# The odd mixer in the program's order: recurrence behind its inputs, two convolution blocks between the transform and its inverse

## The chip, the cores and the metric

One core of one Trainium2 chip runs the whole program. The metric is the time of one execution on the device in microseconds. Five engines with a queue of their own each work through their instructions in order and wait for each other by semaphores: TensorE (PE in the profile; PEld is its weight load), VectorE (DVE), ScalarE (ACT), GpSimd (POOL) and SyncE (SP), which issues the transfers.

## What is computed

A two-layer trunk over 256 latent tokens and 256 context tokens, of width 1024. The change touches the mixer of layer 1, the odd one. Half of its channels are a Hyena operator (a gated long convolution by FFT), half a gated linear recurrence in both directions (RG-LRU). In the reference, cut to the recurrence and the odd mixer:

```python
    for dr in range(2):
        r = jax.nn.sigmoid(... w_a[dr] ...)
        ig = jax.nn.sigmoid(... w_x[dr] ...)
        log_a = -LRU_C * r * jax.nn.softplus(-lam[dr].astype(f32))
        a = jnp.exp(log_a)
        b = jnp.sqrt(-jnp.expm1(2.0 * log_a)) * (ig * xc)
        h = linear_scan(a, b, None if h0 is None else h0[dr], reverse=dr == 1)
        y = h if y is None else y + h
    return (y * jax.nn.gelu(u_gate.astype(f32))).astype(u_x.dtype), finals

def odd_mixer(...):
    hy_l, lx_l, lg_l = jnp.split(h_lat @ w_in, cut, axis=-1)
    r_ctx, ctx_finals = rglru_stream(lx_c, lg_c, *lrup, None, need_ctx_out)
    r_lat, _ = rglru_stream(lx_l, lg_l, *lrup, ctx_finals, True)
    y_lat = jnp.concatenate([hyena_stream(hy_l, *hyp), r_lat], axis=-1) @ w_out
```

The Hyena part takes three groups of 512 channels, each through a convolution of three taps, multiplies the second by the third, convolves the product with a long filter (by a Fourier transform, plus a bias times the product), and multiplies by the first.

## The kernel before

Activations lie with channels on the 128 partitions and tokens along the row: 256 columns of context (CTX) and 256 of latent (LAT), T2 = 512. Every product of matrices is made from three passes (`mm3`, lines 160 to 162): inputs and weights are split into a high and a low part. A weight block of 128x1024 is loaded, cast by ScalarE (L150) and subtracted by VectorE (L151), so each of the 24 matmuls of a block of 1024 input channels has its weight ready.

The odd mixer (`odd_mixer`) begins with a norm and the four blocks of the recurrence's input lx (on both halves of the columns, with the depthwise convolution on ScalarE and VectorE), and goes on with 16 blocks of `od_in` on the latent columns alone: four for the gate lg (Gelu, L1197), 32 single passes for the recurrence's gates (L1207, sigmoid L1208), then eight blocks for the two factors x1 and vv of the product uu (`conv`, L1189 to L1191), whose 128x128 pieces are transposed (L1256), and four blocks for x0. ScalarE copies the transposed product (L1278); 20 passes make the forward transform (L1287 to L1292); VectorE multiplies by the filter's transform (L1294 to L1299, twelve operations); 32 passes make the inverse (L1311), and the result is multiplied by x0 and split into a high and a low part. The eight split tiles, four of the recurrence and four of the Hyena part, are the input of `od_out`, 8 blocks of 24 matmuls.

The recurrence is made from 128x512 operations, four tiles for each direction: tanh (L1216), exp (L1221), square (L1222), VectorE's one-minus (L1223), the gate times lx (L1224), the root (L1229), the input product (L1230), and a scan (L1232 for direction 0; two half scans L1235 and L1236 for direction 1, whose latent half starts from the end of the context half). Each step of it is given to the scheduler at a lower priority (`later`), so a scheduler sorts its operations into the queues between the others by its own estimate.

Memory comes from pools of fixed size with tags: x (8 buffers of 4 KB a row), g (8), lx (2), hy (13), w (4 weight blocks), raw (4), mm (6 PSUM banks). A tile that takes a buffer waits until the tile that held it before was last used.

Of the kernel before, what the change touches and what calls it, by code (L numbers as in the profile page):

```python
# [18 lines left out]
P = 128  # L19
# [43 lines left out]
LN_PARTS = _split3(math.log(2.0), 9, 11)  # L63


class Builder:
# [87 lines left out]
    def mm3(self, ps, w, x, first=True, last=True, keep=False):  # L154
        mm = self.nc.tensor.matmul
# [9 lines left out]
    def split(self, hi, lo, src):  # L165
        self.nc.scalar.copy(hi, src)
        self.nc.vector.tensor_sub(lo, src, hi)
# [343 lines left out]
    def unscaled(self, l, k, xs):  # L511
# [559 lines left out]
    def hyena_prepare(self):  # L1071
# [6 lines left out]
        w1, w2, zt = hp[0:33, 4:68], hp[0:64, 68:132], hp[0:33, 132 : 132 + NTOK]  # L1078
        w3 = self.slot("y", [P, 1024])
# [16 lines left out]
        for j in range(2):  # L1096
# [3 lines left out]
            for d in range(2):  # L1100
                ps = self.ps()
                nc.tensor.matmul(ps, lhsT=h1[:, j * P : (j + 1) * P], rhs=w3[0:64, d * HYC : (d + 1) * HYC], start=True, stop=True)
                e.tensor_mul(fl[:, d, :], ps, dec[:, d, :])
            s = self.slot("y", [P, 2, HYC])
# [56 lines left out]
    def odd_mixer(self):  # L1161
# [7 lines left out]
        cw = self.const([P, 12, 4], "hy_cw", t["hy_cw"])  # L1169
        hb = self.const([P, 4], "hy_b", t["hy_b"])  # L1170
# [15 lines left out]

        def conv(i, o):
            p = self.proj("od_in", i, xs, *LAT)[:, N:T2]
            nc.scalar.activation(o, p, AF.Identity, bias=cw[:, i, 3:4], scale=cw[:, i, 1:2])  # L1189
            v.scalar_tensor_tensor(o[:, 1:N], p[:, 0 : N - 1], cw[:, i, 0:1], o[:, 1:N], op0=ALU.mult, op1=ALU.add)  # L1190
            v.scalar_tensor_tensor(o[:, 0 : N - 1], p[:, 1:N], cw[:, i, 2:3], o[:, 0 : N - 1], op0=ALU.mult, op1=ALU.add)  # L1191
            return o

        lg = self.slot("hy", [P, 4, N])
        for i in range(4):
            ps = self.proj("od_in", 16 + i, xs, *LAT)
            nc.scalar.activation(lg[:, i], ps[:, N:T2], AF.Gelu_apprx_tanh)  # L1197
        gates = {}
        for i in range(4):
            if i % 2 == 0:  # L1200
                wg = self.rawp.tile([P, 2, 4, P], F32, tag="raw", name=self.uid("wg"))
                nc.sync.dma_start(wg, t["lru_w"][:, i : i + 2])
            for d in range(2):
                ra = gates[i, d] = self.slot("g", [P, 2, T2])
                for g in range(2):
                    ps = self.pm()
                    nc.tensor.matmul(ps, lhsT=wg[:, i % 2, 2 * d + g, :], rhs=lx[i], start=True, stop=True)  # L1207
                    nc.scalar.activation(ra[:, g], ps, AF.Sigmoid, bias=lp[:, d, g, i : i + 1])  # L1208

        hs = {}  # L1210

        def recur(d):

            aa = [self.slot("hy", [P, 2, T2]) for _ in range(4)]
            for i in range(4):
                nc.scalar.activation(aa[i][:, 1], gates[i, d][:, 0], AF.Tanh, scale=kap[:, d, i : i + 1])  # L1216
            yield
            for i in range(4):
                a, b = aa[i][:, 0], aa[i][:, 1]
                r, ig = gates[i, d][:, 0], gates[i, d][:, 1]  # L1220
                nc.scalar.activation(a, r, AF.Exp, scale=kap[:, d, i : i + 1])  # L1221
                nc.scalar.activation(r, a, AF.Square)  # L1222
                v.scalar_tensor_tensor(b, r, 1.0, b, op0=ALU.add, op1=ALU.mult)  # L1223
                v.tensor_mul(ig, ig, lx[i])  # L1224
# [356 lines left out]
```

## Time and profile before

| | |
|---|---|
| three runs | 1765.29 (median), 1762.47, 1765.68 us |
| the profiled execution | 1764.04 us, span 1762.0 us, mean granted clock 0.99 |
| TensorE busy | 1702.8 us, 97% of the span |
| VectorE, ScalarE, GpSimd busy | 1267.6 (72%), 693.7 (39%), 13.2 us (1%) |
| the odd mixer, from the first latent block of od_in to the end of od_out | 1439.66 to 1558.2 us |

The page gives the busy time of each engine, then the chain that ended last with the share of each engine, and the costliest groups of instructions. The time line lists single instructions: start, duration, engine, line, operation, output and inputs, and in brackets how long the engine was idle before, and what ended that. Waits are the same brackets summed by line. A row for a stretch gives the busy time of every engine in it.

### The profile page before, as it was taken

How to read it: one execution, taken by the hardware profiler on the slowest of the kernel's cores; microseconds unless marked ns; L12 is line 12 of the kernel's file. 1: busy time of each engine (PE TensorE's matmuls, PEld its weight loads, DVE VectorE, ACT ScalarE, POOL GpSimd, SP SyncE). 2: the span in 40 equal slices, each digit the busy share in tenths (PEclk: the TensorE clock that was granted, in tenths of full speed). 3: DMA queues.
4: the chain of work that ended last, by engine and by line, in shares of the span. 5: the costliest groups of instructions: out<-in, count | busy, mean ns of one | idle time of the engine just before them, and what ended most of it. 6: DMA issues, size and time to landing. Idle time of an engine off the chain costs nothing.

```text
span 1762.0 us, 24867 instructions
## 1 busy us (share of the span) xinstructions
PE 1702.8 (97%) x9380; PEld 1443.5 (82%) x9380; DVE 1267.6 (72%) x2545; ACT 693.7 (39%) x1101; POOL 13.2 (1%) x47
## 2 busy tenths in 40 slices
PE   5999999999989999999999999999999999699998
PEld 3788878889878788778888888888888888499998
DVE  7999999987488668776676686555543576976675
ACT  4433333443445654222222233222222357554443
POOL 0000000000000000000000000000000000000000
PEclk9999999999998999999999999999999999899999
DMA  9566767662465453564554443555533225155552
GB/s 330 172 221 213 228 212 229 215 189 95 126 188 166 132 188 107 171 216 147 164 190 157 159 141 124 181 185 155 169 120 96 96 96 187 67 171 189 183 183 90
DMA packets 107480, 292.65 MB, mean 166 GB/s; under 512 B 21152, under 2 KB 35360, under 8 KB 107104
## 3 DMA queue, kind: packets, MB, share of 16 engines
q1 hardware_dynamic: 101504, 286.86, 50.6%
q10 hardware_dynamic: 5216, 2.62, 0.8%
q0 software_dynamic: 640, 1.57, 0.3%
q8 instruction: 74, 1.21, 0.3%
q14 instruction: 46, 0.38, 0.1%
HBM read 272.20 MB, written 18.28 MB: 165 GB/s over the span
## 4 chain that ended last, share of the span: by engine, by line
PE 89%; DVE 6%; DMA 2%; issue 1%; SPq 1%; ACT 1%; DVEq 0%; ACTq 0%
PE mm L160 25%; PE mm L162 25%; PE mm L161 25%; PE mm L157 7%; DVE w L151 1%; DMA h<-in_modw_dram 1%; PE mm L1207 1%; SPq L1040 1%; DMA x<-d_g 1%; PE mm L907 1%; DVE x L322 0%; DVE nt L315 0%; PE mm L191 0%; PE ps L690 0%; PE ps L1118 0%
## 5 line engine op out<-in xcount | busy, mean ns | idle before, releaser
L150 ACT CAST w<-raw 128x1024 fp32r<-128x1024 f32 (+2 forms) x324 | 328.8, 1019 | 530.6 <-PE mm L162 262.2
L161 PE MATMUL mm<-x,w 128*128 128x512 f32 (+1 forms) x1424 | 519.8, 365 | 0.0
L162 PE MATMUL mm<-x,w 128*128 128x512 f32 (+1 forms) x1424 | 519.2, 365 | 0.0
L160 PE MATMUL mm<-x,w 128*128 128x512 f32 (+1 forms) x1424 | 514.6, 367 | 3.5 <-ACT x L320 2.2
L151 DVE TENSOR_TENSOR w<-raw,w 128x1024 fp32r<-128x1024 f32 (+2 forms) x324 | 383.8, 1186 | 150.5 <-ACT w L150 149.3
L160 PEld LDWEIGHTS mm<-x,w 128*128 128x128 f32 x1424 | 267.4, 189 | 49.5 <-ACT x L320 2.5
L161 PEld LDWEIGHTS mm<-x,w 128*128 128x128 f32 x1424 | 268.6, 189 | 43.8 <-issue 2.0
L162 PEld LDWEIGHTS mm<-x,w 128*128 128x128 f32 x1424 | 268.5, 189 | 43.9 <-issue 1.2
L227 DVE CUSTOM_DVE_ANT_0 junk<-m,sc 128x1024 f32<-128x1024 f32 x224 | 273.0, 1219 | 1.8 <-DMA m<-in_modw_dram 0.4
L160 PE MATMUL mm<-h,w 128*128 128x512 f32 x456 | 178.3, 394 | 0.0
L162 PE MATMUL mm<-h,w 128*128 128x512 f32 x456 | 176.9, 390 | 0.0
L161 PE MATMUL mm<-h,w 128*128 128x512 f32 x456 | 176.7, 390 | 0.0
L435 DVE SCALAR_TENSOR_TENSOR res<-mm,mraw,res 128x256 f32<-128x256 f32 x192 | 86.0, 479 | 96.5 <-PE mm L162 87.2
L471 DVE TENSOR_TENSOR h<-h,mm 128x512 f32<-128x512 f32 x66 | 45.3, 686 | 108.1 <-PE mm L162 95.8
L470 ACT ACTIVATE h<-mm 128x512 f32<-128x512 f32 x66 | 39.5, 598 | 196.0 <-PE mm L162 185.2
L160 PEld LDWEIGHTS mm<-h,w 128*128 128x128 f32 x456 | 85.6, 188 | 18.9 <-issue 1.1
L162 PEld LDWEIGHTS mm<-h,w 128*128 128x128 f32 x456 | 85.6, 188 | 18.5 <-issue 0.6
L161 PEld LDWEIGHTS mm<-h,w 128*128 128x128 f32 x456 | 85.6, 188 | 18.4 <-issue 1.0
L160 PE MATMUL mm<-hy,w 128*128 128x258 f32 x352 | 99.2, 284 | 0.7 <-DVE g L499 0.7
L162 PE MATMUL mm<-hy,w 128*128 128x258 f32 x352 | 99.6, 283 | 0.0
L161 PE MATMUL mm<-hy,w 128*128 128x258 f32 x352 | 99.6, 283 | 0.0
L157 PE MATMUL mm<-x,w 128*128 128x256 f32 x384 | 66.3, 290 | 6.7 <-DVE x L322 6.2
(371 smaller groups left out, 2002.1 us busy)
## 6 DMA issues: line engine op xcount, KB each, us to landing
raw<-in_wgu_dram SPq DMA_DIRECT2D x176, 512.0 KB, 3.9
m<-in_modw_dram SPq DMA_DIRECT2D x130, 512.0 KB, 4.3
raw<-in_wd_dram SPq DMA_DIRECT2D x64, 512.0 KB, 3.6
raw<-in_wd_dram SPq DMA_DIRECT2D x32, 384.0 KB, 3.3
raw<-in_od_in_dram SPq DMA_DIRECT2D x20, 512.0 KB, 3.5
h<-in_modw_dram SPq DMA_DIRECT2D x12, 512.0 KB, 10.0
raw<-in_ev_in_dram SPq DMA_DIRECT2D x10, 512.0 KB, 3.5
d_mb<-mbt SPq DMA_DIRECT2D x16, 256.0 KB, 3.4
```

Source lines behind the costliest of these rows:

```text
L150: nc.scalar.copy(hi[:, :n], raw[:, :n])
L151: nc.vector.tensor_sub(lo[:, :n], raw[:, :n], hi[:, :n])
L157: mm = lambda *a, **k: self.keep(self.nc.tensor.matmul(*a, **k))
L160: mm(ps, lhsT=wh, rhs=xh, start=first and i == 0, stop=False)
L161: mm(ps, lhsT=wh, rhs=xl, start=False, stop=False)
L162: r = mm(ps, lhsT=wl, rhs=xh, start=False, stop=last and i == n - 1)
L227: nc.vector.tensor_tensor_reduce(self.junk, w, self.sc[:, v, :], 1.0, 0.0, ALU.mult, ALU.add, raw[:, dt, v : v + 1])
L435: self.nc.vector.scalar_tensor_tensor(r, ps[:, c0:c1], gate[:, i, VEC[h] : VEC[h] + 1], r, op0=ALU.mult, op1=ALU.add)
L470: nc.scalar.activation(s[:, 0, lo:hi], pg[:, lo:hi], AF.Silu)
L471: nc.vector.tensor_mul(s[:, 1, lo:hi], s[:, 0, lo:hi], pu[:, lo:hi])
L907: nc.tensor.matmul(ps, lhsT=q[0:96, c : c + P], rhs=k[0:96, :nk], start=True, stop=True)
L1040: nc.sync.dma_start(uy[g * 16 : (g + 1) * 16, 1, :].rearrange("p (s n) -> p s n", s=L), d_y[i * 8 + g].rearrange("s c n -> c s n"))
```

## The change

The mixer's operations on ScalarE, VectorE and TensorE go through three objects of a new class `InOrder` (A, V, T). Each adds to every instruction a dependence on the one that was issued through it before, without a semaphore, so that the scheduler keeps the program's order on that engine. Weight casts and subtractions (`wload`) do not go through them and are still sorted in by the scheduler. In the changed kernel all these instructions show line 74.

- The steps of the recurrence become functions (`tanhs`, `exps`, `squares`, `one_minus`, `roots`, `inputs`, `scan`), called at written places between the convolution blocks (`half`) and gate blocks (`gate_proj`). The gates are made in pairs between the blocks, and the gate's Gelu is one 128x1024 activation near the end instead of four.
- The transposed product is copied over `uu` instead of into a tile of its own, right after the first block of x0; the forward transform follows conv(1); conv(2) and conv(3) come between it and the inverse. The squares and exponentials of direction 1 are placed ahead of the transform, its one-minus, roots and input products behind the frequency product.
- The Hyena bias is added to the filter's first tap beforehand, so the result of the inverse is only multiplied by x0.
- The eight split tiles come in four rounds, a tile of the recurrence and one of Hyena each; the rows of `od_out` are stored in that order. The first four blocks of od_out (`first`, `grow`) accumulate two tiles after each round; the other four come at the end as before.
- The two shift columns of the next norm's input are split in `done`, tile by tile.

```diff
+class InOrder:
...
+    def __init__(self, tc, eng):
+        self.tc, self.eng, self.last = tc, eng, None
+    def __getattr__(self, name):
+        def call(*a, **k):
+            ins = getattr(self.eng, name)(*a, **k)
+            if self.last is not None:
+                dep = mybir.DependencyInfo(mybir.DependencyClass.NoSync, mybir.DependencyReason.DATA)
+                self.tc.add_manual_dep(ins.ins, self.last, dep, reason="in order")
+            self.last = ins.ins.name
+            return ins
+        return call
...
-        for i, x in enumerate(xs):
-            self.split(x[:, 0, NTOK : NTOK + 2], x[:, 1, NTOK : NTOK + 2], sh[:, i, 0:1].to_broadcast([P, 2]))
+                self.split(x[:, 0, NTOK : NTOK + 2], x[:, 1, NTOK : NTOK + 2], sh[:, i, 0:1].to_broadcast([P, 2]))
...
+        A, V, T = InOrder(self.tc, nc.scalar), InOrder(self.tc, v), InOrder(self.tc, nc.tensor)
...
+        def gate_proj(i):
+            A.copy(lg[:, i], self.proj("od_in", 16 + i, xs, *LAT, eng=T)[:, N:T2])
...
+        def gate(i):
...
+                    T.matmul(ps, lhsT=self.wg[:, i % 2, 2 * d + g, :], rhs=lx[i], start=True, stop=True)
+                    A.activation(ra[:, g], ps, AF.Sigmoid, bias=lp[:, d, g, i : i + 1])
+                V.tensor_mul(ra[:, 1], ra[:, 1], lx[i])
...
+        def tanhs(d):
...
+                aa[i, d] = self.slot("hy", [P, 2, T2])
+                A.activation(aa[i, d][:, 1], gates[i, d][:, 0], AF.Tanh, scale=kap[:, d, i : i + 1])
...
+        def exps(d):
...
+                A.activation(aa[i, d][:, 0], gates[i, d][:, 0], AF.Exp, scale=kap[:, d, i : i + 1])
+        def squares(d):
...
-        def later(k, low):
-            with self.tc.high_priority(offset=-low):
-                for _ in range(k):
-                    next(lru)
+                A.activation(gates[i, d][:, 0], aa[i, d][:, 0], AF.Square)
+        def one_minus(d):
+            for i in range(4):
+                b = aa[i, d][:, 1]
+                V.scalar_tensor_tensor(b, gates[i, d][:, 0], 1.0, b, op0=ALU.add, op1=ALU.mult)
+        def roots(d):
+            for i in range(4):
+                b = aa[i, d][:, 1]
+                A.activation(b, b, AF.Sqrt, scale=-1.0)
+        def inputs(d, i):
+            b = aa[i, d][:, 1]
+            V.tensor_mul(b, b, gates[i, d][:, 1])
+        def scan(d, i):
+            a, b = aa[i, d][:, 0], aa[i, d][:, 1]
+            hh = hs[i, d] = gates[i, d][:, 0]
+            if d == 0:
+                V.tensor_tensor_scan(hh, a, b, 0.0, op0=ALU.mult, op1=ALU.add)
+                return
+            rv = lambda x, c0, c1: x[:, c0:c1][:, ::-1]
+            V.tensor_tensor_scan(rv(hh, 0, N), rv(a, 0, N), rv(b, 0, N), 0.0, op0=ALU.mult, op1=ALU.add)
+            V.tensor_tensor_scan(rv(hh, N, T2), rv(a, N, T2), rv(b, N, T2), hh[:, 0:1], op0=ALU.mult, op1=ALU.add)
...
+        def half(i, k):
+            if k == 0:
+                self.tm = self.slot("hy", [P, 2, N])
+            conv(4 + 4 * k + i, self.tm[:, k])
+            if k:
+                V.tensor_mul(uu[:, i], self.tm[:, 1], self.tm[:, 0])
...
+        gate_proj(0)
+        gate_proj(1)
+        gate(0)
+        gate(1)
+        half(0, 0)
+        half(0, 1)
+        gate(2)
+        gate(3)
+        half(1, 0)
+        tanhs(0)
+        half(1, 1)
+        turn(0)
+        gate_proj(2)
+        exps(0)
+        half(2, 0)
+        turn(1)
+        squares(0)
+        half(2, 1)
+        gate_proj(3)
+        one_minus(0)
+        half(3, 0)
+        turn(2)
+        roots(0)
+        half(3, 1)
...
         for i in range(4):
-            tm = self.slot("hy", [P, 2, N])
-            x1, vv = conv(4 + i, tm[:, 0]), conv(8 + i, tm[:, 1])
-            v.tensor_mul(uu[:, i], vv, x1)
-            if i:
-                turn(i - 1)
-        later(4, 150)
+            inputs(0, i)
+        tanhs(1)
+        for i in range(4):
+            scan(0, i)
...
-        conv(0, x0[:, 0])
-        conv(1, x0[:, 1])
-        turn(3)
-        ut = self.slot("x", [P, 2, HYC])
-        for j in range(2):
-            nc.scalar.copy(ut[:, j, :], pts[j])
-        conv(2, x0[:, 2])
-        conv(3, x0[:, 3])
         idft = self.slot("hy", [P, 4, N])
         nc.sync.dma_start(idft, t["idft"])
+        conv(0, x0[:, 0])
+        turn(3)
+        ut = uu.rearrange("p (j k) n -> p j (k n)", j=2)
+        for j in range(2):
+            A.copy(ut[:, j, :], pts[j])
+        conv(1, x0[:, 1])
+        exps(1)
+        squares(1)
         yr, yi = self.slot("x", [P, 2, HYC]), self.slot("x", [P, 2, HYC])
...
+        conv(2, x0[:, 2])
+        one_minus(1)
+        conv(3, x0[:, 3])
+        roots(1)
+        A.activation(lg, lg, AF.Gelu_apprx_tanh)
...
+            inputs(1, i)
...
+        def lru_out(i):
+            scan(1, i)
+            h0 = hs[i, 0][:, N:T2]
+            V.tensor_add(h0, h0, hs[i, 1][:, N:T2])
+            V.tensor_mul(lg[:, i], lg[:, i], h0)
...
+            self.split(o[:, 0, N:T2], o[:, 1, N:T2], lg[:, i], A, V)
+            return o
...
+        def hy_ps(i):
...
+                T.matmul(ps[:, :N], lhsT=src, rhs=idft[:, f, :], start=f == 0, stop=f == 3)
+            return ps
+        def hy_out(i, ps):
...
+            V.tensor_mul(z, x0[:, i], ps[:, :N])
...
+            self.split(o[:, 0, N:T2], o[:, 1, N:T2], z, A, V)
+            return o
...
+        gate = self.need(1, 5)
+        os = [None] * 8
+        first = [(self.wload(t["od_out"][b], D), self.pm()) for b in range(4)]
+        def grow(b, k, n=1):
+            w, ps = first[b]
+            self.mm3(ps[:, N:T2], self.wparts(w, KT)[k : k + n], self.parts(os[k : k + n], *LAT), k == 0, k + n == KT, eng=T)
+        zs = [hy_ps(0), hy_ps(1)]
+        for i in range(4):
+            os[2 * i] = lru_out(i)
+            os[2 * i + 1] = hy_out(i, zs[i])
+            if i < 3:
+                for b in range(4):
+                    grow(b, 2 * i, 2)
+            if i < 2:
+                zs.append(hy_ps(i + 2))
+        for b in range(4):
+            grow(b, 6, 2)
...
-        self.out_proj("od_out", 1, os, [LAT])
+        for b in range(4):
+            self.residual(b, first[b][1], gate, LAT, True)
+        for b in range(4, KT):
+            w = self.wload(t["od_out"][b], D)
+            ps = self.pm()
+            self.mm3(ps[:, N:T2], self.wparts(w, KT), self.parts(os, *LAT))
+            self.residual(b, ps, gate, LAT, True)
         self.done = None
...
-    o["od_out"] = wtile(cat([w[512:], w[:512]], axis=0))
+    o["od_out"] = wtile(np.stack([w[512:].reshape(4, P, D), w[:512].reshape(4, P, D)], axis=1).reshape(D, D))
```

Three places as the built programs have them. The first is ScalarE's queue around the copies of the transposed product (ps to x before, ps to hy in the changed kernel); hy_12429 and hy_12443 are x0, hy_12383 to hy_12386 the root tiles of direction 0, g tiles hold gates and scans. Before:

```order
L1229 ACTIVATE hy_12383<-hy_12383 128x512
L1189 ACTIVATE hy_12429<-mm_12506,hy_cw 128x256
L1229 ACTIVATE hy_12384<-hy_12384 128x512
L150 CAST w_12800<-raw_12798 128x1024
L1278 COPY x_12498<-ps_12103 128x512
L1278 COPY x_12498<-ps_12104 128x512
L1229 ACTIVATE hy_12385<-hy_12385 128x512
L1189 ACTIVATE hy_12429<-mm_12539,hy_cw 128x256
L150 CAST w_12836<-raw_12834 128x1024
```

In the changed kernel, with a line of dots for the tanh and weight casts between:

```order
L74 ACT_TABLE_LOAD
L74 ACTIVATE hy_12421<-g_11995,kap 128x512
L74 ACTIVATE hy_12423<-g_12011,kap 128x512
...
L74 ACTIVATE hy_12443<-mm_12451,hy_cb,hy_cw 128x256
L74 COPY hy_11920<-ps_11921 128x512
L74 COPY hy_11920<-ps_11922 128x512
L74 ACTIVATE hy_12443<-mm_12488,hy_cb,hy_cw 128x256
```

The copies stood behind the second block of x0, with two roots of direction 0 still to come; now they stand behind the first one, with all roots ahead of them. x0 (hy_12443) takes the buffer of a tile of direction 0, whose scans stand on VectorE (next place).

The second place is VectorE's queue around the first operations of the frequency product (x<-mm, four of the twelve are shown; SCALAR_TENSOR_TENSOR into g with one input is a scan). Before:

```order
L151 TENSOR_TENSOR w_12836<-raw_12834,w_12836 128x1024
L1230 TENSOR_TENSOR hy_12386<-hy_12386,g_12088 128x512
L1232 SCALAR_TENSOR_TENSOR g_12074<-hy_12385 128x512
L1294 TENSOR_TENSOR x_12569<-mm_12571,hy_12423 128x512
L1191 SCALAR_TENSOR_TENSOR hy_12429<-mm_12539,hy_cw,hy_12429 128x255
L1223 SCALAR_TENSOR_TENSOR hy_12599<-g_12051,hy_12599 128x512
L1232 SCALAR_TENSOR_TENSOR g_12088<-hy_12386 128x512
L1223 SCALAR_TENSOR_TENSOR hy_12600<-g_12065,hy_12600 128x512
L1295 TENSOR_TENSOR x_12579<-mm_12572,hy_12424 128x512
L1297 TENSOR_TENSOR x_12570<-mm_12571,hy_12424 128x512
```

In the changed kernel:

```order
L74 SCALAR_TENSOR_TENSOR g_12089<-hy_12159 128x512
L74 SCALAR_TENSOR_TENSOR g_12105<-hy_12161 128x512
L169 TENSOR_TENSOR w_12641<-raw_12639,w_12641 128x1024
L74 SCALAR_TENSOR_TENSOR hy_12443<-mm_12451,hy_cw,hy_12443 128x255 x2
L74 SCALAR_TENSOR_TENSOR hy_12443<-mm_12488,hy_cw,hy_12443 128x255 x2
L74 TENSOR_TENSOR x_12524<-mm_12526,hy_12437 128x512
L74 TENSOR_TENSOR x_12534<-mm_12527,hy_12438 128x512
L169 TENSOR_TENSOR w_12647<-raw_12645,w_12647 128x1024
L74 TENSOR_TENSOR x_12524<-x_12524,x_12534 128x512
L74 TENSOR_TENSOR x_12525<-mm_12526,hy_12438 128x512
L74 TENSOR_TENSOR x_12534<-mm_12527,hy_12439 128x512
L169 TENSOR_TENSOR w_12653<-raw_12651,w_12653 128x1024
```

Scans of direction 0 and one-minus operations of direction 1 (hy_12599, hy_12600) stood between the products; now all scans stand ahead, the taps of x0's first two blocks follow, and then come the products with two weight subtractions between them. The x tiles that the products write (x_12524, x_12525, x_12534) take buffers of the eight x tiles that are the input of conv(2) and conv(3) on TensorE.

The third place is VectorE's queue at the output tiles: g_12051 and others are the half scans of direction 1, hy_11917 (hy_11919) the gate lg, hy_12664 (hy_12674) the product with x0, and the split's subtraction writes g or x. Before:

```order
L1236 SCALAR_TENSOR_TENSOR g_12095<-hy_12602,g_12095 128x256
L1238 TENSOR_TENSOR g_12058<-g_12058,g_12065 128x256
L1238 TENSOR_TENSOR g_12074<-g_12074,g_12081 128x256
L1303 TENSOR_TENSOR hy_11917<-hy_11917,g_12044 128x256
L1238 TENSOR_TENSOR g_12088<-g_12088,g_12095 128x256
L1303 TENSOR_TENSOR hy_11917<-hy_11917,g_12058 128x256
L1313 SCALAR_TENSOR_TENSOR hy_12664<-hy_12102,hy_b,mm_12659 128x256
L1303 TENSOR_TENSOR hy_11917<-hy_11917,g_12074 128x256
L1313 SCALAR_TENSOR_TENSOR hy_12675<-hy_12102,hy_b,mm_12670 128x256
L1313 SCALAR_TENSOR_TENSOR hy_12686<-hy_12102,hy_b,mm_12681 128x256
L1303 TENSOR_TENSOR hy_11917<-hy_11917,g_12088 128x256
L167 TENSOR_TENSOR g_12644<-hy_11917,g_12644 128x256
```

In the changed kernel, the first round and the start of the second:

```order
L74 SCALAR_TENSOR_TENSOR g_11995<-hy_12421 128x256
L74 SCALAR_TENSOR_TENSOR g_11995<-hy_12421,g_11995 128x256
L74 TENSOR_TENSOR g_11987<-g_11987,g_11995 128x256
L74 TENSOR_TENSOR hy_11919<-hy_11919,g_11987 128x256
L74 TENSOR_TENSOR g_12671<-hy_11919,g_12671 128x256
L74 TENSOR_TENSOR hy_12674<-hy_12443,mm_12657 128x256
L74 TENSOR_TENSOR x_12676<-hy_12674,x_12676 128x256
L74 SCALAR_TENSOR_TENSOR g_12011<-hy_12423 128x256
L74 SCALAR_TENSOR_TENSOR g_12011<-hy_12423,g_12011 128x256
```

The steps of the four tiles stood beside each other; now a tile's scans, addition, product and subtraction follow each other, then Hyena's product and subtraction, and then the next tile's. Each subtraction needs ScalarE's cast of the operation before it.

## Rows read from the trace of the kernel before

**Rows 1.** The page: chain that ended last, share of the span by engine
```profile
PE 89%; DVE 6%; DMA 2%; issue 1%; SPq 1%; ACT 1%; DVEq 0%; ACTq 0%
```

**Rows 2.** Busy us (PE, PEld, DVE, ACT, POOL), clock, DMA, GB/s by stretch
```profile
1439.66:1499.90 60.24, 60.24 (x421) 52.41 (x419) 40.33 (x58) 45.56 (x64) 0.00 (x0) 1.00 0.58 195
1499.90:1514.00 14.10, 10.32 (x21) 4.29 (x20) 14.10 (x20) 13.99 (x22) 0.00 (x0) 0.88 0.42 147
1514.00:1538.70 24.70, 14.74 (x63) 12.52 (x63) 24.69 (x59) 8.96 (x24) 0.00 (x0) 0.79 0.00 1
1538.70:1558.20 19.50, 19.50 (x165) 19.50 (x164) 14.50 (x24) 12.24 (x21) 0.00 (x0) 1.00 0.47 143
```

**Rows 3.** What TensorE waited for, 1437 to 1562: us, times, longest
```profile
PE mm L1311 <- DVE x L1296: 6.2, 1, 6.2
PE mm L1287 <- ACT x L1278: 3.7, 1, 3.7
PE mm L160 <- ACT g L166: 2.6, 1, 2.6
```

**Rows 4.** Time line of TensorE in the odd mixer: start, duration
```profile
1451.54 13.04 PE L1207 MATMUL mm<-lx,wg 128*128 128x512 f32 x30
...
1503.68 2.07 PE L1287 MATMUL mm<-x,hy 128*128 128x512 f32 x2 [3.71 <-ACT x L1278]
...
1535.54 0.41 PE L161 MATMUL mm<-g,w 128*128 128x256 f32 x1
1535.75 0.41 PE L162 MATMUL mm<-g,w 128*128 128x256 f32 x1
```

**Rows 5.** VectorE by line and shape, 1437 to 1562: busy us, mean ns
```profile
L151 DVE TENSOR_TENSOR w<-raw,w 128x1024 fp32r<-128x1024 f32 x27 | 32.8, 1220 | 5.0 <-ACT w L150 5.0
...
L1190 DVE SCALAR_TENSOR_TENSOR hy<-mm,hy_cw,hy 128x255 f32<-128x255 f32 x12 | 5.8, 479 | 11.3 <-ACT hy L1189 11.3
...
L1230 DVE TENSOR_TENSOR hy<-hy,g 128x512 f32<-128x512 f32 x8 | 5.4, 680 | 0.0
...
L1232 DVE TENSOR_TENSOR_SCAN g<-hy 128x512 f32<-128x512 f32 x4 | 4.9, 1216 | 0.0
...
L1236 DVE TENSOR_TENSOR_SCAN g<-hy,g 128x256 f32<-128x256 f32 x4 | 2.8, 730 | 0.0
L1235 DVE TENSOR_TENSOR_SCAN g<-hy 128x256 f32<-128x256 f32 x4 | 2.6, 672 | 0.0
...
L167 DVE TENSOR_TENSOR g<-hy,g 128x256 fp32r<-128x256 f32 x4 | 1.7, 419 | 0.0
```

**Rows 6.** ScalarE by line and shape, same stretch
```profile
L150 ACT CAST w<-raw 128x1024 fp32r<-128x1024 f32 x26 | 27.0, 1042 | 7.4 <-PE mm L162 7.4
...
L1189 ACT ACTIVATE hy<-mm,hy_cw 128x256 f32<-128x256 f32 x12 | 6.7, 560 | 10.9 <-PE mm L162 10.9
...
L1229 ACT ACTIVATE hy<-hy 128x512 f32<-128x512 f32 x8 | 5.0, 630 | 3.0 <-DVE hy L1223 3.0
...
L166 ACT CAST x<-hy 128x256 fp32r<-128x256 f32 x4 | 1.6, 406 | 1.2 <-DVE hy L1314 1.0
...
L1278 ACT COPY x<-ps 128x512 f32<-128x512 f32 x2 | 1.1, 587 | 0.0
```

**Rows 7.** Time line of VectorE, single operations of the odd mixer
```profile
1447.96 0.74 DVE L1182 SCALAR_TENSOR_TENSOR lx<-mm,lru_cw,lx 128x510 f32<-128x510 f32 x1
...
1515.26 0.68 DVE L1297 TENSOR_TENSOR x<-mm,hy 128x512 f32<-128x512 f32 x1
1515.86 0.68 DVE L1298 TENSOR_TENSOR x<-mm,hy 128x512 f32<-128x512 f32 x1
...
1538.27 0.42 DVE L167 TENSOR_TENSOR x<-hy,x 128x256 fp32r<-128x256 f32 x1
```

**Rows 8.** Time line of ScalarE around one table load
```profile
1487.83 1.33 ACT L1216 ACTIVATE hy<-g,kap 128x512 f32<-128x512 f32 x2
1489.15 1.28 ACT L1221 ACT_TABLE_LOAD   x1
```

More of the change, by code (lines that the diff above doesn't have):

```diff
@@ L152, in wload, with mm3 @@
         return hi, lo
-    def mm3(self, ps, w, x, first=True, last=True, keep=False):
-        mm = self.nc.tensor.matmul
+    def mm3(self, ps, w, x, first=True, last=True, keep=False, eng=None):
+        mm = (eng or self.nc.tensor).matmul
         if keep:
@@ L163, in mm3, with split @@
         return r
-    def split(self, hi, lo, src):
-        self.nc.scalar.copy(hi, src)
-        self.nc.vector.tensor_sub(lo, src, hi)
+    def split(self, hi, lo, src, act=None, dve=None):
+        (act or self.nc.scalar).copy(hi, src)
+        (dve or self.nc.vector).tensor_sub(lo, src, hi)
     def mod_fix(self, l, m, raw, src, i0, i1):
@@ L1185, in odd_mixer @@
             lx.append(xc)
+        A, V, T = InOrder(self.tc, nc.scalar), InOrder(self.tc, v), InOrder(self.tc, nc.tensor)
         def conv(i, o):
[L1188 to L1191, printed above, removed]
+            p = self.proj("od_in", i, xs, *LAT, eng=T)[:, N:T2]
+            A.activation(o, p, AF.Identity, bias=cb[:, i : i + 1], scale=cw[:, i, 1:2])
+            V.scalar_tensor_tensor(o[:, 1:N], p[:, 0 : N - 1], cw[:, i, 0:1], o[:, 1:N], op0=ALU.mult, op1=ALU.add)
+            V.scalar_tensor_tensor(o[:, 0 : N - 1], p[:, 1:N], cw[:, i, 2:3], o[:, 0 : N - 1], op0=ALU.mult, op1=ALU.add)
             return o
         lg = self.slot("hy", [P, 4, N])
-        for i in range(4):
-            ps = self.proj("od_in", 16 + i, xs, *LAT)
-            nc.scalar.activation(lg[:, i], ps[:, N:T2], AF.Gelu_apprx_tanh)
+        def gate_proj(i):
+            A.copy(lg[:, i], self.proj("od_in", 16 + i, xs, *LAT, eng=T)[:, N:T2])
         gates = {}
-        for i in range(4):
+        def gate(i):
             if i % 2 == 0:
-                wg = self.rawp.tile([P, 2, 4, P], F32, tag="raw", name=self.uid("wg"))
-                nc.sync.dma_start(wg, t["lru_w"][:, i : i + 2])
+                self.wg = self.rawp.tile([P, 2, 4, P], F32, tag="raw", name=self.uid("wg"))
+                nc.sync.dma_start(self.wg, t["lru_w"][:, i : i + 2])
             for d in range(2):
@@ L1206, in odd_mixer @@
                     ps = self.pm()
[L1207 to L1214, printed above, removed]
+                    T.matmul(ps, lhsT=self.wg[:, i % 2, 2 * d + g, :], rhs=lx[i], start=True, stop=True)
+                    A.activation(ra[:, g], ps, AF.Sigmoid, bias=lp[:, d, g, i : i + 1])
@@ L1306, in odd_mixer @@
-            os.append(o)
-        for i in range(4):
+            self.split(o[:, 0, N:T2], o[:, 1, N:T2], lg[:, i], A, V)
+            return o
+        def hy_ps(i):
             ps = self.pm()
```

73 lines of the change are left out of this document (21 added, 52 removed).

## The prediction

> **What bounds the kernel now.** I read first the chain of waits: TensorE carries 89% of what ended last [rows 1]. So a microsecond counts where TensorE has to wait, or runs at half clock. The busy time by stretch then shows the odd mixer as four stages [rows 2]. From 1439.66 to 1499.90 TensorE never stops. In the two middle stages, 38.8 us long, TensorE is busy for 25.1 us and VectorE (DVE in the rows) for 38.79, that is, all the time. In the last one, 19.50 us, TensorE is full again. The waits of TensorE name the three large holes [rows 3]: 3.7 us for the copies of the transposed product (L1278) ahead of the forward transform, 6.2 us for the frequency product (L1296) ahead of the inverse, 2.6 us for the first split tile of the recurrence (L166) ahead of od_out. What runs right behind a hole is at half clock: the mean granted clock of the two middle stages is 0.88 and 0.79 [rows 2], and od_out's matmuls at 1535.5 follow each other at 0.21 us [rows 4], against 19.50 / 165 = 0.12 in the last stage. Without any hole the work would be 16 od_in blocks of 24 x 0.12 = 2.88 (46.1), 32 gate passes of 13.04 / 30 = 0.43 (13.8), 0.6 of transposes, 20 forward passes at 0.43 (8.6), 32 inverse ones at 0.215 (6.9), 8 od_out blocks of 2.88 (23.0): 99.0 of the 118.5 us, so 19.5 us are the most that can be won.
>
> **The change, part by part.** Ahead of the odd mixer the order of every engine is as before, but for one addition on a 1x512 row and one small load while the filter is prepared. Nothing waits for them, and I price them at nothing (at most one VectorE operation of 0.68 [rows 5]). TensorE does the same matmuls. The work that goes is four bias operations on VectorE of 0.48 each and two table loads of ScalarE (ACT in the rows). What matters is that each engine now takes the mixer's operations strictly in the program's order, and which buffers these take. Three places follow.
>
> First, **the forward transform**. ScalarE's copies of the transposed product now stand behind the activation that opens x0, and x0 takes a "hy" buffer which the inputs of the recurrence's first direction hold: it is free only when VectorE has run the fourth scan. I walk there on before's clock. The eleventh block (half(3, 0)) ends on TensorE at 1439.66 + 11 x 2.88 + 32 gates (13.4 by starts) + 0.3 of transposes + about 1.3 for PSUM banks behind the lx chain, which ends at 1447.96 + 0.74 [rows 7]: 1486.3. The roots stand behind it: ScalarE does an activation 0.56, a cast 0.95 net, a table load 1.28, four roots at 0.63 less 0.1 of overlap, and the next activation 0.56 [rows 6, 8]: 1491.8. VectorE then does two taps (1.0), the product uu (0.42), four input products at 0.60, four scans and two weight splits at 1.22 less 0.09 (6.8) [rows 5]: 1502.4. The 0.60 is the distance of two independent operations of 0.68 in [rows 7]. ScalarE's activation (0.45 net) and first copy (0.59) [rows 6] bring the transform to 1503.5, where before it began at 1503.68 [rows 4]. So moving it up in the program gains nothing, though TensorE meets it two blocks earlier and now waits 7 to 8 us there instead of 3.7 (three blocks of 2.88 from 1486.3 end at 1495.1). I take no change; my walk may be off by 1.5 us either way.
>
> Second, **the two convolution blocks**. The transform lasts 10.2 us, cold start included, as before: 1513.8. Then come the blocks conv(2) and conv(3), 2.88 each, which should hide the frequency product. But that product's results yr, yi and the scratch tile take "x" buffers, and all eight of these hold the mixer's input until conv(3) has read it tile by tile. So VectorE's first product waits for the third matmul of conv(3): 1513.8 + 2.88 + 0.5 = 1517.2. From about 1506 to 1517.2 VectorE has nothing that it may do, as the second direction of the recurrence stands behind the products. Before, it did 11 us of taps, scans and inputs there [rows 2]. Behind 1517.2 stand 12 products (12 x 0.60 + 0.2), two weight splits (2.3), four taps (1.8), and four 1 - a² operations and four inputs at 0.60 (4.8) [rows 5, 7]: 16.3 us, to 1533.5.
>
> Third, **the output rounds**. In each of four rounds VectorE does two half scans (0.67 + 0.73), an addition (0.41) and a product (0.42), waits for ScalarE's cast (0.41), subtracts (0.42), multiplies by x0 (0.42), waits for a cast (0.41), subtracts (0.42): 4.31, about 4.4 with the hand-overs [rows 5, 6]. Before, the same operations of the four tiles were interleaved, so that VectorE never waited for a cast. Strictly in order nothing fills these. Without the two waits, and with overlap, it would be 2.9. I take 4.4, since every step needs the one before; four rounds 17.6 us, so the last split tile comes at 1551.1, where before it came at 1538.7 [rows 7]. What is gained is behind it: three quarters of four od_out blocks are done by then, so 21 matmuls (2.5), about 0.4 for the fifth block's weight, whose slot the first block frees, and four blocks (11.5) are left: 14.4 instead of 19.5 us. End: 1565.6 against 1558.1, **+7.5 us**.
>
> The profiled execution took 1764.04 us (span 1762.0), and with it the sum is 1771.5. The median of the runs is 1765.29, 1.25 above it; 1765.3 + 7.5 = 1772.8, so I say **1773**. Bounds: the start of the transform -1.5 to +1.5, the rounds -6.0 (2.9 each) to +1.6 (4.8 each, with a bubble of 0.2 at each hand-over), half clock in the rounds 0 to +5.
>
> A rule of the Trainium skill gives the table load another price: "ScalarE: Activation LUTs", section What ACT_TABLE_LOAD costs, puts it at 1.28 us and a drain of 1.38. Here a load of 1.28 begins at 1489.15, right where the activation before it ends (1487.83 + 1.33) [rows 8], so no drain is seen ahead of it; by the page one load on the path would add 1.4, to 1774.4.
>
> **The rivals.** (b) TensorE stays at half clock in the rounds. For it: behind the 2.6 us hole of before the matmuls ran at 0.21 [rows 3, 4], and in the rounds TensorE waits about 1 us in each and 10 us ahead of the first. A round's 24 matmuls then take 5.1 and the inverse 0.4 or more: three rounds at 5.5 instead of 4.4, and 21 x 0.09 at the end: +5.2, **1778**. Against it: the stretch from 1537.2 on was warm with short holes just before.
>
> (c) The rounds cost 2.9: ScalarE's casts overlap with VectorE's next operations. That is 6.0 less, +1.5: **1766.8**, no measurable change. For it: ScalarE is idle there, busy for 8.96 of 24.70 us [rows 2]. Against it: VectorE's order is fixed, and the subtraction stands right behind the cast that it needs.
>
> (d) Not slower but a little faster: VectorE doesn't stand still from 1506 to 1517.2, because the products don't wait for conv(3)'s buffers. Its 33.9 us of work (16.3 + 17.6) then run from 1506 to 1539.9, and + 14.4 gives 1554.3: 3.8 less than 1558.1, **1761.5**. It decides from the point where more than 7.5 of the 33.9 us are done before 1517.2. Against it: the buffers' owners, as read from the order and the pools. The Trainium skill speaks for it in "Perfetto Trace Analysis", section Optimization Strategy: where the most contended engine changes over time, interleaving the regimes may improve performance. Here it does change, from TensorE to VectorE at 1499.9 and back at 1538.7 [rows 2], and by the page the convolution blocks inside VectorE's stage should pay.
>
> **How the numbers follow.** The forecast 0.56, (b) 0.12, (c) 0.16, (d) 0.16. A change of 0.2% (3.5 us) is about what the measurement can tell from none: same is 1761.8 to 1768.8. Nearly all of (d) is faster, since it may come out larger if the rounds are shorter too: 0.14. Same is (c) and the rest of (d): 0.18. Slower is the forecast and (b): 0.68. The range from 1764 to 1780 holds the forecast with its bounds, (b), and most of (c); it leaves out (d) and the lower edge of (c), about 2 in 10.
>
> **What would show it.** In the profile after: TensorE waits 7 to 8 us for the copies ahead of the forward transform, which starts within 1.5 us of 1503.5; the first scan of direction 0 to the fourth stand ahead of the activation that opens x0; VectorE is idle for about 11 us until the third matmul of conv(3); four rounds of about 4.4 us, with two waits for ScalarE each; about 14.4 us from the last split tile to the end of od_out. I am wrong if VectorE is busy while the convolution blocks run, or if a round takes less than 3.5 us, or if the time before the mixer moves.

## The result and the profile after

The changed kernel takes **1774.26 us** (median; 1772.72 to 1774.74) against 1764.78 of the kernel before in the same comparison: 9.5 us more, a ratio of 1.0054 (95% interval 1.0037 to 1.0072). The forecast was 1773. The profiled execution took 1772.72 us, with a span of 1770.9 us, 8.9 us more than before's 1762.0.

What TensorE waited for, from the odd mixer's start to the program's end, in the changed kernel (us in total, times, longest):

```profile
PE mm L74 <- ACT hy L74: 6.9, 1, 6.9
PE mm L74 <- ACT g L74: 5.2, 1, 5.2
PE mm L74 <- DVE x L74: 4.8, 2, 3.6
PE mm L178 <- DVE g L517: 2.3, 1, 2.3
PE ps L74 <- DVE hy L74: 0.7, 1, 0.7
```

These answer to [rows 3]. The hole ahead of the forward transform (copies, ACT hy) grew from 3.7 to 6.9 us; the one ahead of the inverse (products, DVE x) shrank from 6.2 to 4.8, since the two convolution blocks stand in it; the one ahead of od_out (first split tile, ACT g) grew from 2.6 to 5.2. A fourth one, of 2.3 us, lies in the next stage, where the kernel before waited 0.7:

```profile
PE mm L160 <- DVE g L499: 0.7, 1, 0.7
```

Busy time by stretch, the changed kernel (start:end, sum, then PE, PEld, DVE, ACT, POOL, the granted clock, DMA share, GB/s), to be held against [rows 2]:

```profile
1439.73:1495.80 56.07, 55.13 (x373) 46.63 (x371) 40.41 (x59) 45.41 (x66) 0.00 (x0) 1.00 0.51 169
1495.80:1512.80 17.00, 10.08 (x21) 4.37 (x20) 8.88 (x11) 8.49 (x15) 0.00 (x0) 0.80 0.59 194
1512.80:1533.10 20.30, 13.24 (x66) 10.45 (x64) 16.26 (x27) 9.06 (x11) 0.00 (x0) 0.83 0.16 52
1533.10:1550.90 17.80, 14.89 (x91) 13.86 (x92) 13.61 (x30) 3.34 (x9) 0.00 (x0) 0.81 0.00 1
1550.90:1565.00 14.10, 14.07 (x117) 13.86 (x117) 13.27 (x28) 11.76 (x25) 0.00 (x0) 1.00 0.58 177
```

Before, VectorE was busy all the time between TensorE's two full stretches (38.79 of 38.8 us). Now these middle stages last 55.1 us and VectorE is busy for 38.75 of them: about as much work, with 16 us of standing still in between. Where, its time line shows (start, duration; in brackets how long it was idle before, and what ended that):

```profile
1501.65 1.20 DVE L169 TENSOR_TENSOR w<-raw,w 128x1024 fp32r<-128x1024 f32 x1
1502.76 2.03 DVE L74 SCALAR_TENSOR_TENSOR hy<-mm,hy_cw,hy 128x255 f32<-128x255 f32 x4
1516.70 1.29 DVE L74 TENSOR_TENSOR x<-mm,hy 128x512 f32<-128x512 f32 x2 [11.91 <-PE mm L74]
...
1533.06 0.68 DVE L74 TENSOR_TENSOR_SCAN g<-hy 128x256 f32<-128x256 f32 x1
1533.78 0.75 DVE L74 TENSOR_TENSOR_SCAN g<-hy,g 128x256 f32<-128x256 f32 x1
1534.56 0.42 DVE L74 TENSOR_TENSOR g<-g,g 128x256 f32<-128x256 f32 x1
1535.09 0.42 DVE L74 TENSOR_TENSOR hy<-hy,g 128x256 f32<-128x256 f32 x1
1535.99 0.42 DVE L74 TENSOR_TENSOR g<-hy,g 128x256 fp32r<-128x256 f32 x1 [0.47 <-ACT g L74]
1536.33 0.41 DVE L74 TENSOR_TENSOR hy<-hy,mm 128x256 f32<-128x256 f32 x1
1537.21 0.43 DVE L74 TENSOR_TENSOR x<-hy,x 128x256 fp32r<-128x256 f32 x1 [0.47 <-ACT x L74]
...
1550.51 0.43 DVE L74 TENSOR_TENSOR x<-hy,x 128x256 fp32r<-128x256 f32 x1 [0.40 <-ACT x L74]
```

11.91 us pass ahead of the first product, which TensorE's matmul ends (the third of conv(3)), and in a round two waits of 0.47 us end with ScalarE's casts. The transform's hole begins on ScalarE:

```profile
1494.87 2.92 ACT L168 CAST w<-raw 128x1024 fp32r<-128x1024 f32 x3
1501.76 0.56 ACT L74 ACTIVATE hy<-mm,hy_cb,hy_cw 128x256 f32<-128x256 f32 x1 [3.98 <-DVE g L74]
1502.23 1.06 ACT L74 COPY hy<-ps 128x512 f32<-128x512 f32 x2
```

The activation that opens x0 waits 3.98 us for a scan (g) of VectorE, and the copies stand behind it.

### The profile page after: what moved, and what is told of

Its sections match the earlier page's. It is cut to its first block, busy times and chain, and to the rows that moved or that the text cites. A ratio compares the mean times of both kernels' runs of the same rounds, so it can differ in the third digit from the quotient of the medians.

```text
span 1770.9 us, 24866 instructions
## 1 busy us (share of the span) xinstructions
PE 1705.3 (96%) x9380; PEld 1444.4 (82%) x9380; DVE 1268.8 (72%) x2542; ACT 692.3 (39%) x1100; POOL 13.2 (1%) x47
## 4 chain that ended last, share of the span: by engine, by line
PE 89%; DVE 6%; ACT 2%; DMA 1%; issue 1%; SPq 1%; DVEq 0%; ACTq 0%
PE mm L178 24%; PE mm L180 24%; PE mm L179 24%; PE mm L175 7%; PE mm L74 4%; DVE w L169 1%; DMA h<-in_modw_dram 1%; DVE hy L74 1%; PE mm L924 1%; DVE x L340 0%; DVE nt L333 0%; ACT w L168 0%; PE mm L976 0%; SPq L1057 0%; PE mm L209 0%
## 5 line engine op out<-in xcount | busy, mean ns | idle before, releaser
L179 PE MATMUL mm<-x,w 128*128 128x512 f32 (+1 forms) x1280 | 479.2, 375 | 0.0
L180 PE MATMUL mm<-x,w 128*128 128x512 f32 (+1 forms) x1280 | 478.4, 374 | 0.0
L178 PE MATMUL mm<-x,w 128*128 128x512 f32 (+1 forms) x1280 | 473.7, 376 | 3.5 <-ACT x L338 2.2
L178 PEld LDWEIGHTS mm<-x,w 128*128 128x128 f32 x1280 | 240.1, 189 | 49.0 <-ACT x L338 2.5
L179 PEld LDWEIGHTS mm<-x,w 128*128 128x128 f32 x1280 | 241.2, 188 | 43.7 <-issue 1.8
L180 PEld LDWEIGHTS mm<-x,w 128*128 128x128 f32 x1280 | 241.1, 188 | 43.2 <-issue 1.0
```

The costliest lines, as they stand in the source:

```text
L178: mm(ps, lhsT=wh, rhs=xh, start=first and i == 0, stop=False)
L179: mm(ps, lhsT=wh, rhs=xl, start=False, stop=False)
L180: r = mm(ps, lhsT=wl, rhs=xh, start=False, stop=last and i == n - 1)
```

## The experiments

Eight kernels. The odd mixer begins up to 3 us earlier or later on the time line from one execution to the next, with the stages ahead of it. So stretches inside the mixer are compared by their distance from the last pair of transposes (1492.62 in the changed kernel), and times by the medians beside the kernel before (in brackets behind a ratio its 95% interval). The changed kernel was not run again beside the experiments, and the medians of the kernel before differ between the comparisons (1764.78, 1765.6 and 1765.4), so "less than the changed kernel" is uncertain by about 1 us. The traces agree with these differences: from the last transposes to the end of od_out it is 72.7 us in the changed kernel, 66.0 with the copies first, 65.8 with buffers of their own, 61.6 with both.

**Copies first.** The changed kernel; the two copies ahead of x0's activation:

```diff
-        conv(0, x0[:, 0])
+        p0 = self.proj("od_in", 0, xs, *LAT, eng=T)[:, N:T2]
         turn(3)
...
             A.copy(ut[:, j, :], pts[j])
+        taps(0, x0[:, 0], p0)
```

> The changed kernel with one order undone: ScalarE's two copies of the transposed product stand ahead of the activation that opens x0, so they no longer wait for the buffer that direction 0's scans hold. Theory (the hole ahead of the forward transform is the wait of the copies for that buffer): the transform starts at about 1498 instead of 1502.9 (behind tanh and two weight casts on ScalarE), VectorE's first product at about 1511.5 instead of 1516.7, and the time falls by 5 us, to about 1769. Rival (VectorE's scans set the pace, and the transform is not on the path): the transform moves but the products do not, and the time stays within 1 us of 1774.

Measured: 1766.97 us, 1.0008 of before (0.9999 to 1.0018), 7.3 less than the changed kernel. The transform starts 4.7 us behind the transposes instead of 10.2. TensorE's time line:

```profile
1494.36 0.44 PE L74 MATMUL ps<-ident,hy 128*128 128x128 f32 x2 [0.74 <-DVE hy L74]
1499.10 8.85 PE L74 MATMUL mm<-hy,hy 128*128 128x512 f32 x20 [1.44 <-ACT hy L74]
```

And VectorE's, at the first product:

```profile
1511.22 1.29 DVE L74 TENSOR_TENSOR x<-mm,hy 128x512 f32<-128x512 f32 x2 [4.82 <-PE mm L74]
```

The theory holds, and about 2 us more came than the 5 expected: the transform starts 5.5 us earlier instead of 4.9, and it became 1.7 us shorter, 8.85 us behind a hole of 1.44, where in the changed kernel it took 10.58 behind 6.92. So the hole costs twice: as a wait, and as half clock behind it.

**Buffers of their own for the products.** The changed kernel with

```diff
-        yr, yi = self.slot("x", [P, 2, HYC]), self.slot("x", [P, 2, HYC])
+        yr, yi = self.slot("lx", [P, 2, HYC]), self.slot("lx", [P, 2, HYC])
...
-            tm = self.slot("x", [P, 2, HYC])
+            t0, t1 = gates[2 * f, 0][:, 1], gates[2 * f + 1, 0][:, 1]
```

> The changed kernel with the frequency product written elsewhere: yr and yi in the two buffers of lx, which are free by then, and the scratch in the gate halves of direction 0, so that no product waits for the input tiles that conv(3) reads. Nothing else moves in the program; the scheduler puts the two weight splits a little later. Theory: VectorE's 11.9 us of idling ahead of the products shrink to about 3; they begin at about 1505 to 1508, the rounds begin at about 1526.4 instead of 1533.1, and the time falls by 6.7 us, to about 1767.6. Rival (the late start of the transform alone is the loss; the work of VectorE behind it is limited by conv(3)'s taps): the rounds begin less than 2 us earlier.

Measured: 1766.55 us, 1.0008 of before (0.9999 to 1.0017), 7.7 less than the changed kernel. VectorE:

```profile
1506.94 0.69 DVE L74 TENSOR_TENSOR lx<-mm,hy 128x512 f32<-128x512 f32 x1 [1.81 <-PE mm L74]
1510.37 0.69 DVE L74 TENSOR_TENSOR g<-mm,hy 128x512 f32<-128x512 f32 x1 [2.74 <-PE mm L74]
...
1526.48 0.68 DVE L74 TENSOR_TENSOR_SCAN g<-hy 128x256 f32<-128x256 f32 x1
```

11.9 us of idling became 4.6, now for the transform's own results, and the rounds begin 33.5 us behind the transposes, 6.9 earlier than in the changed kernel (6.7 expected).

**Both.** The two edits together.

> Both edits together: copies first, and the products in buffers of their own. Theory: VectorE is busy from the scans on, with one wait of some 1 to 3 us for the weight casts that stand behind the activations of conv(2) and conv(3); the rounds begin at about 1522.6, 10.4 us earlier than 1533.1, and the time falls to about 1764, the same as the kernel before. If the two holes were one and the same loss, it would be no faster than the better of the two alone (about 1767.6).

Measured: 1763.04 us, 0.9984 of before (0.9975 to 0.9993): 11.2 less than the changed kernel. TensorE still waits 8.0 us for the first split tile, but the rounds begin 28.3 us behind the transposes instead of 40.4. The two holes are two losses in a row. They do not simply add (7.3 + 7.7 = 15.0), since both fill the same idle time of VectorE; once it is full (from the taps to the rounds it has no wait left), nothing more comes from there.

**Rounds without waits for casts.** The changed kernel; in a round both casts come first, then the next tile's scans, then both subtractions:

```diff
             os[2 * i] = lru_out(i)
-            os[2 * i + 1] = hy_out(i, zs[i])
+            os[2 * i + 1], z = hy_out(i, zs[i])
+            if i < 3:
+                lru_scan(i + 1)
+            V.tensor_sub(os[2 * i][:, 1, N:T2], lg[:, i], os[2 * i][:, 0, N:T2])
+            V.tensor_sub(os[2 * i + 1][:, 1, N:T2], z, os[2 * i + 1][:, 0, N:T2])
```

> The changed kernel with another order inside the output rounds only: both casts of a round are issued before the two subtractions, and the next tile's two half scans stand between them, so VectorE does not stand at a cast. Theory: a round takes about 3.1 us on VectorE instead of 4.43 and the last split tile comes at about 1546 instead of 1550.9; TensorE's 24 matmuls and the inverse of a round (2.9 + 0.9 us) then limit two rounds, so that the time falls by 2.5 us only, to about 1771.8 (by 4.7 if TensorE keeps up). Rival (TensorE's rate in the rounds is the limit already, its clock included): the split tiles come earlier and the time does not change.

Measured: 1774.84 us, 1.0048 of before (1.0031 to 1.0065): no change. The theory's expectation failed and the rival's holds: the last split tile comes 0.8 us earlier (57.5 against 58.3 us behind the transposes, where 5 us were expected), and nothing comes of it. VectorE, third round:

```profile
1544.14 0.42 DVE L74 TENSOR_TENSOR g<-g,g 128x256 f32<-128x256 f32 x1
1544.59 0.42 DVE L74 TENSOR_TENSOR hy<-hy,g 128x256 f32<-128x256 f32 x1
1547.01 0.42 DVE L74 TENSOR_TENSOR hy<-hy,mm 128x256 f32<-128x256 f32 x1 [1.99 <-PE mm L74]
```

The wait for a cast is replaced by a wait for the inverse: the third tile's inverse stands behind 24 matmuls of od_out in TensorE's order, and these ran at half clock in the first round. VectorE's waits for casts were real but not alone: TensorE's inverse and 24 matmuls of a round take 4.6 us even at full clock (in the changed kernel from 1541.41 to 1546.01), where the expectation has 3.8. The edit has a price of its own as well: the first subtraction stands behind two scans, TensorE waits 1.0 us for it, and its first 24 matmuls end 0.9 us later than in the changed kernel (49.7 against 48.8 us behind the transposes). The end of od_out comes later by just as much (73.6 against 72.7), since TensorE has no hole in between. So here TensorE sets the end; what rounds without casts would win without that delay was not run.

**No written-out partial blocks.** The changed kernel without `first` and `grow`: eight plain od_out blocks behind the rounds.

```diff
-        first = [(self.wload(t["od_out"][b], D), self.pm()) for b in range(4)]
...
-        for b in range(4, KT):
+        for b in range(KT):
```

> The changed kernel without the four written-out partial blocks: od_out is eight plain blocks behind the rounds, sorted by the scheduler (which itself interleaves three blocks tile by tile, since three PSUM banks are free). Theory: what the partial blocks win is small, one more block's 18 matmuls (2.2 us) ahead of the last tile, and part of it is lost in the next stage, where the statistics stand behind 74 matmuls (69 here): 0.5 to 1.5 us slower than the changed kernel, about 1775. Rival (the partial blocks win the 5 us by which the tail of the changed kernel is shorter than before's): about 1779.

Measured: 1773.67 us, 1.0047 of before (1.0033 to 1.0061). No slower; the 0.5 to 1.5 us that were expected did not show. The scheduler lets three blocks grow by itself, so the four written-out ones win nothing that can be measured.

**Shift columns back.** The changed kernel with the splits of the shift columns out of `done`, and ahead of the output tiles.

```diff
-                self.split(x[:, 0, NTOK : NTOK + 2], x[:, 1, NTOK : NTOK + 2], sh[:, i, 0:1].to_broadcast([P, 2]))
...
+        for i, x in enumerate(xs):
+            self.split(x[:, 0, NTOK : NTOK + 2], x[:, 1, NTOK : NTOK + 2], sh[:, i, 0:1].to_broadcast([P, 2]))
```

> The changed kernel with the shift-column splits back ahead of the output tiles instead of in done. The scheduler then puts the statistics of the next norm behind 68 matmuls of the next block instead of 74. Theory (TensorE's wait of 2.3 us at 1586, against 0.7 before, comes from that place in TensorE's queue): the wait falls by 0.7 us, to about 1.6. Rival (the chain of VectorE behind the statistics sets it): it stays at 2.3.

Measured: 1774.0 us, 1.0049 of before (1.0035 to 1.0062); TensorE's wait is 2.3 us as in the changed kernel. The place of the statistics in TensorE's queue is not what sets it.

**Hyena tiles first.** Both edits, and the rounds in another order (cut):

```diff
+        for i in range(4):
+            V.tensor_mul(z4[:, i], x0[:, i], zps[i])
+            o = os[2 * i + 1] = self.slot("x", [P, 2, T2], F32R)
+            A.copy(o[:, 0, N:T2], z4[:, i])
         A.activation(lg, lg, AF.Gelu_apprx_tanh)
         for i in range(4):
...
+            V.tensor_sub(o[:, 1, N:T2], z4[:, i], o[:, 0, N:T2])
+            for b in range(4):
+                grow(b, 2 * i + 1)
+        for i in range(4):
             inputs(1, i)
...
+        scan(1, 0)
```

> Both edits of e3_both, and the output rounds in another order: direction 1's one-minus right behind the products, then the four Hyena tiles (all four inverse results in two PSUM banks, four multiplications, four casts, four subtractions), which TensorE adds to the first four od_out blocks while VectorE does direction 1's input products and scans; then the four tiles of the recurrence, the next tile's scans standing between a cast and its subtraction. Theory (VectorE's round trips to ScalarE and TensorE's late start in the rounds are what is left): the last split tile comes at about 1535.8 on the time line, where e3_both has it at 1539.7, behind it stand 12 matmuls and four blocks instead of 21 to 24 and four; the end of od_out falls by 4.6 us against e3_both, to about 1758.4, which is 0.4% below the kernel before. Rival (as in e4_rounds, TensorE limits the end and not the split tiles): 1762 to 1764, as e3_both.

Measured: **1757.73 us**, 0.996 of before (0.9947 to 0.9974), 0.7 from the expected time. TensorE:

```profile
1520.71 5.90 PE L74 MATMUL mm<-x,w 128*128 128x256 f32 x47 [0.67 <-DVE x L74]
1526.93 0.38 PE L74 MATMUL mm<-g,w 128*128 128x256 f32 x1 [0.33 <-ACT g L74]
1528.20 1.69 PE L74 MATMUL mm<-g,w 128*128 128x256 f32 x12 [0.89 <-DVE g L74]
```

While VectorE does the input products and the first scans, TensorE adds the four Hyena tiles to four blocks. No hole in the mixer is longer than 1.4 us, and the granted clock is 1.00 from the transform to the end of od_out. The last split tile stands 42.0 us behind the transposes, against 46.2 with the two edits alone.

**The same with the shift columns back.**

> e7_hyena_first with the shift-column splits put back ahead of the output tiles (out of done), as the kernel before has them. The scheduler then puts the matmuls of the next norm's statistics behind 65 instead of 68 matmuls of the next block. Theory: 0.3 to 0.8 us less than e7_hyena_first. Rival: no difference.

Measured: **1756.38 us**, 0.9949 of before (0.9936 to 0.9961), 1.35 less than without. That is more than expected, though the single times of the two kernels still touch (1755.61 to 1756.86, and 1756.32 to 1761.68); clearer is TensorE's wait in the next stage, 0.7 us as in the kernel before instead of 2.3. VectorE in the changed kernel, where that wait ends (it is the same without this edit):

```profile
1584.37 1.22 DVE L169 TENSOR_TENSOR w<-raw,w 128x1024 fp32r<-128x1024 f32 x1 [0.92 <-ACT w L168]
1585.51 0.42 DVE L517 TENSOR_TENSOR g<-mm,g 128x256 f32<-128x256 f32 x1
```

and here:

```profile
1569.36 0.16 DVE L519 COPY bias<-mm 128x1 f32<-128x1 f32 x1 [1.02 <-PE mm L180]
1569.53 0.42 DVE L517 TENSOR_TENSOR g<-mm,g 128x256 f32<-128x256 f32 x1
1569.87 0.42 DVE L520 TENSOR_TENSOR g<-mm,g 128x256 f32<-128x256 f32 x1
```

In the changed kernel a weight subtraction, waiting for its cast, stands ahead of the product with the next norm's factor (L517), for which TensorE waits; here it stands behind, as in the kernel before (product at 1576.78, subtraction at 1578.78). The scheduler sorts it one way or the other when some short operations near it move. That the order of these two is the whole of the 1.6 us is read from the rows; it was not swapped by itself.

## Why the prediction was right

Step by step, as the prediction has them on before's clock, and as the changed kernel's time line shows them:

| step | predicted | measured |
|---|---|---|
| the eleventh block ends on TensorE | 1486.3 | 1485.7 |
| ScalarE's activation behind the roots ends | 1491.8 | 1491.1 |
| forward transform starts | 1503.5 | 1502.86 |
| transform ends | 1513.8 | 1512.87 |
| first product on VectorE | 1517.2 | 1516.70 |
| first round starts | 1533.5 | 1533.06 |
| a round | 4.4 | 4.47 |
| last split tile | 1551.1 | 1550.94 |
| from there to the end of od_out | 14.4 | 14.4 |
| end of od_out | 1565.6 | 1565.3 |
| time behind the mixer | 0 | +1.6 |

The sum did not come out by large errors that cancel: from one step to the next, up to the end of od_out, prediction and measurement differ by 0.6 us at most, and that is at the start.

- **The two buffers.** Both waits that the prediction read from the order and the pools are there. Each was taken away by itself and gave back 7.3 and 7.7 us; without both the change is a small gain (0.9984). So the loss is not in the idea of putting convolution blocks between the transform and its inverse but in what the written order waits for. The wait for the copies was 6.9 us where the prediction says 7 to 8 (its own figures, 1495.1 and 1503.5, give 8.4): the transform began 0.6 us earlier and TensorE came 0.8 later, with a wait of 0.7 ahead of the last transposes that the walk leaves out. The rule that the prediction cites from the Trainium skill ("Perfetto Trace Analysis", section Optimization Strategy), that interleaving stages with different bounds may pay, is not contradicted by the runs once the buffers are free, at 0.9984 and 0.996; what the interleaving alone is worth no run shows, since these kernels keep the other parts of the change.
- **Why 0.6 us early.** The transform began 0.6 us ahead of the walk, because the walk began 0.6 us too late: the eleventh block ended at 1485.7 instead of 1486.3. Of the 1.3 us that the walk allows for PSUM banks, an estimate, about 0.6 are there. From that block to the transform it is 17.2 us in both. Two weight subtractions stand ahead of the last scan's end, as the walk has them, and ScalarE's activation starts right at that end.
- **The table load.** The page that the prediction weighs ("ScalarE: Activation LUTs" of the Trainium skill, section What ACT_TABLE_LOAD costs) adds a drain of 1.38 us to each load; that the sum with it, 1774.4, lies nearer to the measured 1774.26 than the forecast is chance. Again no drain is seen: ScalarE's time line has the load right behind the activation, and the next activation right behind the load, so the walk without it stood:

```profile
1490.53 0.55 ACT L74 ACTIVATE hy<-mm,hy_cb,hy_cw 128x256 f32<-128x256 f32 x1
1491.10 1.28 ACT L74 ACT_TABLE_LOAD   x1
1492.39 2.56 ACT L74 ACTIVATE hy<-g,kap 128x512 f32<-128x512 f32 x4
```

- **The rounds.** Their length was right, and there was luck in it: the prediction takes it from VectorE alone, and TensorE was as long about it. From its first matmul of od_out at 1536.01 to the end TensorE does not wait any more; a round's inverse (eight matmuls, 1.5 us, for which rival (b) puts "0.4 or more") and 24 matmuls take it 4.6 us, and it comes to the last split tile just as that is ready:

```profile
1541.41 1.89 PE L74 MATMUL mm<-hy,x 128*128 128x256 f32 x8
1546.01 1.89 PE L74 MATMUL mm<-hy,x 128*128 128x256 f32 x8
1550.97 0.53 PE L74 MATMUL mm<-x,w 128*128 128x256 f32 x3
```

  So the price of rival (c) would have been wrong: with VectorE's waits for casts gone the rounds took as long, since TensorE's inverse was next. The prediction did not look at what is queued ahead of the inverse on TensorE; the expectation of that run did, at too low a price.
- **Rival (b), half clock in the rounds,** came true for the first one: its 24 matmuls, from 1536.0 to 1541.4, ran at a granted clock of 0.58. Here it cost nothing that can be seen, since TensorE was in time for the last split tile (1550.97 against 1550.94), and from the second round on the clock was full. With both edits it did cost: there the first 24 matmuls ran at 0.50, and from the last split tile to the end of od_out it is 15.4 us instead of 14.4. The argument for this rival reads the trace of before wrongly in one point: behind its hole of 2.6 us three matmuls still ran at full clock, and half clock began at 1534.0, behind two more holes of 0.3 and 0.7 us.
- **Rival (d)** was priced at 1761.5 for products that wait for nothing. With only their buffers free the time was 1766.55: VectorE then waited 4.6 us for the transform's results, which the price left out.
- **The term that was missing** is the stage behind the mixer. The prediction takes the time from the end of od_out on as unchanged. The span grew by 8.9 us, of which 7.2 are in the mixer (1565.3 against 1558.1) and 1.6 are the fourth hole, 2.3 instead of 0.7 us. With it the sum would have been +9.1, next to the measured 9.5. Why the scheduler sorts that stage otherwise behind the changed mixer stays open.

## What to carry to other kernels

A written order is only as good as the buffers that its operations take: ask of each moved operation which tile it overwrites, who reads that tile last, and what stands behind the waiting instruction on its engine. When a wait is taken away, look up what is queued ahead of the next thing that the engine needs, on the other engine too; here the wait for a cast only changed into a wait for a matmul. And compare the scheduler's order behind the changed stage as well, since a weight subtraction that slips ahead of one product went with 1.6 of the 9.5 us.

## What the runs showed of the hardware

Half clock follows the long holes of this mixer and not the short ones. Two stretches of the changed kernel right behind its holes of 6.9 and 5.2 us (columns as in the table by stretch above; the clock is the third figure from the end):

```profile
1502.86:1512.87 10.01, 10.01 (x20) 4.39 (x21) 1.82 (x4) 5.41 (x10) 0.00 (x0) 0.82 0.41 167
1536.00:1541.40 5.40, 5.39 (x24) 4.78 (x25) 4.13 (x9) 1.00 (x3) 0.00 (x0) 0.58 0.01 3
```

and the transform of the kernel with the copies first, behind a hole of 1.4 us:

```profile
1499.10:1507.60 8.50, 8.50 (x21) 3.91 (x21) 7.23 (x9) 5.48 (x10) 0.00 (x0) 1.00 0.97 347
```

The 24 matmuls that took 5.4 us take 2.88 at full clock. So a long hole cost TensorE 1.5 to 2.5 us beyond its length, which reaches the end only where TensorE is the one that others wait for. Behind the five holes of 0.3 to 0.9 us in the rounds of the kernel with the Hyena tiles first the clock stayed at 1.00.

In between it can come out either way. The hole of the next stage is 2.28 us long in all eight kernels that have it, such as

```profile
1585.98 0.39 PE L178 MATMUL mm<-hy,w 128*128 128x258 f32 x1 [2.28 <-DVE g L517]
```

in the changed kernel, where the granted clock of the next 3 us is 1.00, as it is in four other profiled executions. In three it is not: 0.50 with the copies first, 0.53 with both edits, 0.76 with the Hyena tiles first. What decides it stays open. A hole that is brought down to the sizes that left the clock at 1.00 here (1.4 us and less) can be worth more than the microseconds it loses, and one execution does not show what a hole of 2.3 us costs.
